# w_down of a squared-ReLU MLP: a seven-product scheme over four pairs of k tiles instead of three, a fifth product that passes from bank to bank, and results added to h by DMA

## The chip, the cores and the metric

The kernel runs on one core of a Trainium2 chip. The metric is device time in microseconds (us) of one execution. TensorE (PE) multiplies, VectorE (DVE) and ScalarE (ACT) do elementwise work, GpSimd (POOL) does little here and issues a few transfers, SyncE (SP) issues the weight loads.

## The reference

A transformer block of width 2048 on 256 rows, in float32. The mixer has two branches (a recurrence and a chunked attention), merged by gates. What the change touches is the MLP behind it, whose hidden width is 8192:

```python
def reference(x, w_in, ..., w_up, w_down, norm_final_w):
    h = x
    h = h + mixer_block(rms_norm(h, norm_mix_w[l]), ..., w_out[l])
    u = rms_norm(h, norm_mlp_w[l])
    h = h + jnp.square(jax.nn.relu(u @ w_up[l])) @ w_down[l]
    return rms_norm(h, norm_final_w)
```

`w_up` is 2048 x 8192, `w_down` is 8192 x 2048.

## The kernel before

**Numbers.** Every float32 operand is split into a high and a low part: `split` (L87) lets ScalarE copy the source into the high part (L89, a cast) and VectorE subtract it from the source (L90). A product of one 128 x 128 block with a 128 x 512 weight tile is then three matmuls of 512 columns (`mm3`, L143 to L145): high by high, high by low, low by high. They add up in a PSUM bank of 128 x 512.

**The MLP.** The hidden width is worked off in four quarters (`qd`, 0 to 3). In a quarter two gemms of 1024 columns each (`up{qd}0`, `up{qd}2`) make the 2048 hidden columns; ScalarE takes each bank through a ReLU and a square. `turn` transposes the results (`tp_u` on TensorE) and splits them into `uT`, tiles named act_u. Then two gemms, `dn{qd}0` and `dn{qd}2`, multiply by the quarter's 2048 rows of w_down, 1024 output columns each, and `out_of` adds each bank to the running sum `h1` (named h in the profile) with one VectorE addition, `evict` (L677). In the last quarter the final norm follows.

**A gemm.** `gemm_s` computes two blocks of 128 rows by two blocks of 512 columns, over 16 k tiles. Four banks `c["11"]`, `c["21"]`, `c["12"]`, `c["22"]` hold the four results. For some pairs of k tiles (k with k+4; r of them) a 2 x 2 by 2 x 2 block product is made with seven products in place of eight, after Winograd. The weight side needs sums of weight blocks, made in place in the raw tiles by VectorE (`add`, L698); the activation side needs combinations S2, S4, S5 and S7, made once for a quarter by `combos`. Products 1 to 7 go to banks, and parts of them move between banks: ScalarE copies a bank (`copy`, L722) to another bank or to a token (a 128 x 512 buffer), and VectorE adds a token to a bank (`more`, L727). The remaining k tiles are plain products, by pairs: `plain` loads 2 tiles of 512 columns and multiplies them by both row blocks.

With r = 3, weight tiles W11, W12, W21, W22 hold two k tiles each, and the third pair lies in X and Y, made of halves. All w_down gemms, w_up gemms (but the first) and gate gemms use r = 3, two others r = 2.

**The order.** Instructions are put in order by a scheduler before the run; each engine then runs its own list in order. `late` and `flush` carry the last plain pair and the last results of a gemm (12 matmuls) into the middle of the next. `turns`, passed as `between`, puts the transposes of the second half of the hidden columns into the first w_down gemm of a quarter.

**Buffers.** A raw weight tile of 128 x 1024 float32 (512 KB) is loaded by one or two DMAs on SyncE's queue (`piece`, L641 and L644). `parts` makes the high and low tiles `wh` and `wl` from it. Raw tiles have eight buffers, 6 in one pool and 2 in another, taken in turn; `wh` and `wl` have six each, by 4 and 2:

```python
BUFS = {"raw": (6, 2), "wh": (4, 2), "wl": (4, 2)}
...
    first = taken[tag] % (old + new) < old
    taken[tag] += 1
```

A raw buffer comes free when the last operation that reads it, mostly a split on VectorE, is done. There are 17 tokens (`TOK`), six PSUM banks for `gemm_s` and two for transposes.

In the names of the profile `wh_dn20p` is the high part of a weight tile for a product of gemm dn20, `wh_dn20r` that of a plain pair, `raw_dn` and `raw_dn20r` the tiles loaded for them, `S_u` an activation combination.

Of the kernel before, what the change touches and what calls it, by code (L numbers as in the profile page):

```python
# [8 lines left out]
F32 = mybir.dt.float32  # L9
F32R = mybir.dt.float32r  # L10
# [6 lines left out]
P = 128  # L17
# [5 lines left out]
NC = 512  # L23
# [27 lines left out]
def tile_hybrid_block(  # L51
# [529 lines left out]

    R = 3

    def combos(lhs, what, home):

        a = []
        for m in range(NM):
            for j in range(2):
                t = tk.tile([P, R, P], F32, name=f"a{m}{j}_{what}", tag="t", bufs=TOK)
                x = lhs[j][:, :R, :, m * P:(m + 1) * P].bitcast(F32)  # L590
                nc.vector.tensor_tensor(t, x[:, :, 0, :], x[:, :, 1, :], op=ALU.add)
                a.append(t)
        a11, a12, a21, a22 = a
        s5 = a22
        nc.vector.tensor_tensor(s5, a21, a22, op=ALU.subtract)
        s7 = a21
        nc.vector.tensor_tensor(s7, a11, a21, op=ALU.subtract)
        s2 = a11
        nc.vector.tensor_tensor(s2, s5, a11, op=ALU.subtract)
        s4 = a12  # L600
        nc.vector.tensor_tensor(s4, a12, s2, op=ALU.add)
        made = {}
        for i, s in ((4, s4), (5, s5), (2, s2), (7, s7)):
            t = (tk if home == "a" else xp).tile([P, R, 2, P], F32R, name=f"S{i}_{what}", tag=f"S{i}{home}", bufs=1)
            split(t[:, :, 0, :], t[:, :, 1, :], s)
            made[i] = t
        return made

    Sx = combos(xT, "x", "a")
# [66 lines left out]
        with tc.high_priority(offset=2000):  # L676
            nc.vector.tensor_tensor(dst, acc, dst, op=ALU.add)  # L677

    def gemm_s(lhs, S, w, n0, what, done, r=R, kt0=0, between=None, fresh=False, tail=False):

        n1 = n0 + NC
        c = {}
        load = lambda name, *halves: piece(w, f"{what}{name}", *[(n, kt0 + k) for n, k in halves])
        W11 = load("11", (n0, 0), (n0, 1))
        if r == 3:
            X = load("x", (n0, 2), (n1, 6))
        W22 = load("22", (n1, 4), (n1, 5))  # L690
        W12 = load("12", (n1, 0), (n1, 1))
        if r == 3:
            Y = load("y", (n0, 6), (n1, 2))
        W21 = load("21", (n0, 4), (n0, 5))

        def add(dst, t):
            with tc.high_priority(offset=2000):
                nc.vector.tensor_tensor(dst, dst, t, op=ALU.add)  # L698

        half = lambda W, i: W[0][:, i * NC:(i + 1) * NC]  # L700

        def mm(i, lh, ps, *tiles):

            first = i not in c
            if first:
                c[i] = bank(f"{what}c{i}")
            wh, wl = ps
            for a, k in tiles:
                mm3(c[i], *lh(k), wh[:, a], wl[:, a], first, False)
                first = False  # L710

        def of(m, jj):
            return lambda k: lhs_of(lhs, k + 4 * jj, m)

        def comb(i):
            return lambda k: [S[i][:, k, u, :] for u in range(2)]

        both = ((0, 0), (1, 1))

        def copy(dst, i):  # L720
            with tc.high_priority(offset=2000):
                nc.scalar.copy(dst, c[i])  # L722
            return dst

        def more(i, t, op):
            with tc.high_priority(offset=2000):
                nc.vector.tensor_tensor(c[i], c[i], t, op=op)  # L727


        p = parts(W11, f"{what}p1")  # L730
        if r == 3:
            px = parts(X, f"{what}px")
        mm("11", of(0, 0), p, *both)
        if r == 3:
            mm("11", of(0, 0), px, (0, 2))
        c["21"] = bank(f"{what}c21")
        if fresh:
            nc.tensor.matmul(c["21"], lhs[0][:, 0, 0, 0:P], lhs[0][:, 0].rearrange("p u t -> p (u t)"), start=True, stop=False, skip_group_check=True)
        copy(c["21"], "11")
        p = parts(W22, f"{what}p3")  # L740
        add(W22[0], W12[0])
        add(W12[0], W11[0])
        mm("12", comb(4), p, *both)
        if r == 3:
            mm("12", comb(4), px, (1, 2))

        p = parts(W12, f"{what}p5")
        mm("22", comb(5), p, *both)
        if r == 3:
            add(half(X, 1), half(Y, 1))  # L750
            add(half(Y, 1), half(X, 0))
            py = parts(Y, f"{what}py")
            mm("22", comb(5), py, (1, 2))
        more("12", copy(token(f"s5_{what}"), "22"), ALU.add)
        if r == 3:
            mm("11", of(0, 1), py, (0, 2))
        p = parts(W21, f"{what}p2")
        mm("11", of(0, 1), p, *both)
        add(W11[0], W22[0])
        flush()  # L760

        p = parts(W11, f"{what}p6")
        mm("21", comb(2), p, *both)
        if r == 3:
            add(half(X, 0), half(X, 1))
            px = parts(X, f"{what}px2")
            mm("21", comb(2), px, (0, 2))
        u1 = copy(token(f"u1_{what}"), "21")

        def plain(n, *ks):  # L770
            p = parts(load(f"r{n}_{ks[0]}", *[(n0 + n * NC, k) for k in ks]), f"{what}r{n}_{ks[0]}")

            def m_half(m):
                for a, k in enumerate(ks):
                    mm3(c["12"[m] + "12"[n]], *lhs_of(lhs, k, m), p[0][:, a], p[1][:, a], False, k == KD - 1)

            return m_half

        def plains(n, *pairs):
            for ks in pairs:  # L780
                p = plain(n, *ks)
                for m in range(NM):
                    p(m)


        left = [(k, k + 1) for k in range(2, KD, 2) if k != 4] if r == 2 else [(3, 7)] + [(k, k + 1) for k in range(8, KD, 2)]
        plains(1, left[0])
        more("12", u1, ALU.subtract)
        p = parts(W22, f"{what}p7")
        mm("21", comb(7), p, *both)  # L790
        if r == 3:
            mm("21", comb(7), px, (1, 2))
        u2 = copy(token(f"u2_{what}"), "21")
        add(W21[0], W11[0])
        early = left[1][1] // 4 < len(lhs)
        if early:
            plains(1, left[1])
        else:
            q = plain(0, *left[0])
            q(0)  # L800
        more("22", u2, ALU.subtract)
        p = parts(W21, f"{what}p4")
        mm("21", of(1, 1), p, *both)
        if r == 3:
            add(half(Y, 0), half(X, 0))
            mm("21", of(1, 1), parts(Y, f"{what}p4y", 0), (0, 2))
        if not early:
            q(1)
        if between:
            between()  # L810

        def end(n):
            for m in range(NM):
                done(m, n, c["12"[m] + "12"[n]])

        plains(0, *left[0 if early else 1:2])
        plains(1, *left[2 if early else 1:2])
        for n in range(2):
            plains(n, *left[2:-3])
        plains(0, *left[max(2, len(left) - 3):])  # L820
        end(0)
        if tail:
            held = [plain(1, *ks) for ks in left[-3:]]
            for m in range(NM):
                for p in held:
                    p(m)
                done(m, 1, c["12"[m] + "2"])
            return
        plains(1, *left[-3:-1])

        def rest():
            plains(1, left[-1])
            end(1)

        late.append(rest)
# [79 lines left out]
    for qd in range(NQ):  # L915
# [4 lines left out]
        def turn():  # L920

            c, rs = pend.pop(0)
            uT.append(new_act(f"u{qd}{c}"))
            hi, lo = uT[-1][:, :, 0, :], uT[-1][:, :, 1, :]
            for m in range(NM):
                tp = transpose4(rs[m], f"u{qd}{c}{m}")
                split(hi[:, :, m * P:(m + 1) * P], lo[:, :, m * P:(m + 1) * P], tp)

        Su = {}

        def turns():
            if len(hT) == 2:
                h_blocks(2)
            while pend:
                turn()
            if len(uT) == 2:
                Su.update(combos(uT, f"u{qd}", "b"))

        for c in range(0, 4, 2):
            rs = {}  # L940
# [14 lines left out]

        def out_of(m, n, acc, last=last):
            r = h1[n][m]
            evict(r, acc)
            if not last:
                return  # L960
            nc.scalar.activation(token(f"ysq_{n}_{m}"), r, AF.Square, accum_out=ssq3[:, m, n:n + 1])
            if n < 3:
                nc.vector.tensor_tensor(r, r, wf[:, n * NC:(n + 1) * NC], op=ALU.mult)
# [12 lines left out]
                (nc.sync if i % 2 else nc.scalar).dma_start(out[m * P:(m + 1) * P, i * NC:(i + 1) * NC], t)  # L976

        for n0 in (0, 2):
            gemm_s(uT, Su, w_down, n0 * NC, f"dn{qd}{n0}", lambda m, n, acc, n0=n0: out_of(m, n0 + n, acc), kt0=qd * KD,
                   between=None if n0 else turns, tail=last and n0 == 2)  # L980


# [42 lines left out]
```

## Time and profile before

| | |
|---|---|
| median of 3 runs | 1426.92 us (1425.85 to 1427.75) |
| the profiled execution | 1427.14 us |
| span of its profile | 1425.4 us |
| mean granted TensorE clock | 0.996 |
| moved by DMA | 272.89 MB |

The span is what the profile sees of one execution; 1.7 us of that execution's time lie around it. Engine times are busy times within the span; a gap of an engine costs time only where the rest waits for it. In rows of groups the columns after the bar are the group's busy time in us and the mean ns of one; in rows of windows, the window, its length, and the busy us and count of instructions of each engine, then the clock, the DMA share and GB/s; in rows of the chain, the start, the length and what ran.

### The profile page before, as it was taken

The numbers are of one execution on the slowest core, as the hardware profiler recorded it, in microseconds if no ns is written. First come the engines' busy times: TensorE is split into PE (matmuls) and PEld (weight loads), VectorE is DVE, ScalarE is ACT, GpSimd is POOL, SyncE is SP. The second block draws the span as 40 slices with busy tenths as digits, with TensorE's granted clock in tenths as the row PEclk, the third lists the DMA queues.
The fourth block names the chain that finished last, engine by engine and source line by source line (L and its number), as shares of the span: only waits on it lengthen the run. The fifth ranks groups of instructions, "written<-read, shape, count | busy, mean of one in ns | idle before, by whom it ended". The sixth has DMA issues, their size and how long they took to land.

```text
span 1425.4 us, 18422 instructions
## 1 busy us (share of the span) xinstructions
PE 1404.7 (99%) x6629; PEld 1163.1 (82%) x6629; DVE 1153.9 (81%) x1522; ACT 849.0 (60%) x1105; POOL 35.5 (2%) x96
## 2 busy tenths in 40 slices
PE   9999999999999999999999999999999999999997
PEld 7878888878787888888888888888888888888886
DVE  7797978675658885688998988889888898889984
ACT  6754844464556664446656765567556775557753
POOL 2000001010000000000000000000000000000000
PEclk9999999999999999999999999999999999999999
DMA  9644554655556557666654576555576555667542
GB/s 327 222 148 147 163 166 142 188 170 168 174 177 221 195 192 228 196 207 222 200 181 134 194 236 209 176 201 169 192 236 232 179 171 170 237 222 237 179 151 99
DMA packets 122156, 272.89 MB, mean 191 GB/s; under 512 B 10176, under 2 KB 31424, under 8 KB 121680
## 3 DMA queue, kind: packets, MB, share of 16 engines
q1 hardware_dynamic: 119328, 264.80, 56.1%
q0 software_dynamic: 1584, 5.31, 1.4%
q10 hardware_dynamic: 1152, 1.60, 0.3%
q8 instruction: 52, 0.85, 0.2%
q14 instruction: 40, 0.33, 0.1%
HBM read 269.57 MB, written 2.10 MB: 191 GB/s over the span
## 4 chain that ended last, share of the span: by engine, by line
PE 83%; DVE 8%; ACT 3%; DMA 3%; issue 2%; POOL 0%; SPq 0%; POOLq 0%; ACTq 0%; DVEq 0%
PE acc_hq L171 2%; PE acc_ak L171 2%; PE acc_aq L171 2%; PE acc_hf L171 2%; PE ps L395 1%; PE acc_bb L143 1%; PE acc_av L144 1%; PE acc_ba L145 1%; PE acc_ba L144 1%; PE acc_ba L143 1%; PE acc_bb L144 1%; PE acc_av L143 1%; PE acc_bb L145 1%; PE acc_av L145 1%; PE acc_ak L170 1%
## 5 line engine op out<-in xcount | busy, mean ns | idle before, releaser
L171 PE MATMUL acc_hf<-act_x,wh_hf 128*128 128x512 f32 x128 | 47.7, 408 | 0.0
L171 PE MATMUL acc_aq<-act_x,wh_aq 128*128 128x512 f32 x128 | 47.5, 406 | 0.0
L171 PE MATMUL acc_hq<-act_x,wh_hq 128*128 128x512 f32 x128 | 46.3, 401 | 0.0
L171 PE MATMUL acc_ak<-act_x,wh_ak 128*128 128x512 f32 x128 | 45.0, 397 | 0.0
L698 DVE TENSOR_TENSOR raw_up<-raw_up,raw_up 128x1024 f32<-128x1024 f32 x32 | 39.0, 1220 | 0.5
L698 DVE TENSOR_TENSOR raw_dn<-raw_dn,raw_dn 128x1024 f32<-128x1024 f32 x32 | 39.0, 1217 | 0.2
L90 DVE TENSOR_TENSOR wl_ga<-raw_ga,wh_ga 128x1024 fp32r<-128x1024 f32 x16 | 19.6, 1225 | 19.6 <-ACT wh_ga L89 18.1
L170 PE MATMUL acc_aq<-act_x,wl_aq 128*128 128x256 f32 x120 | 35.1, 292 | 0.0
L170 PE MATMUL acc_hf<-act_x,wl_hf 128*128 128x256 f32 x120 | 34.5, 287 | 0.0
L90 DVE TENSOR_TENSOR wl_av<-raw_av,wh_av 128x1024 fp32r<-128x1024 f32 x16 | 19.6, 1224 | 18.1 <-ACT wh_av L89 18.1
L170 PE MATMUL acc_ak<-act_x,wl_ak 128*128 128x256 f32 x120 | 33.6, 280 | 0.0
L170 PE MATMUL acc_hq<-act_x,wl_hq 128*128 128x256 f32 x120 | 33.6, 280 | 0.0
L90 DVE TENSOR_TENSOR wl_ba<-raw_ba,wh_ba 128x1024 fp32r<-128x1024 f32 x16 | 19.6, 1223 | 16.6 <-ACT wh_ba L89 16.6
L90 DVE TENSOR_TENSOR wl_bb<-raw_bb,wh_bb 128x1024 fp32r<-128x1024 f32 x16 | 19.5, 1222 | 14.7 <-ACT wh_bb L89 14.7
L89 ACT CAST wh_ba<-raw_ba 128x1024 fp32r<-128x1024 f32 x16 | 16.9, 1053 | 24.3 <-PE acc_ba L145 10.0
L89 ACT CAST wh_bb<-raw_bb 128x1024 fp32r<-128x1024 f32 x16 | 16.9, 1055 | 22.8 <-PE acc_ba L145 12.7
L89 ACT CAST wh_av<-raw_av 128x1024 fp32r<-128x1024 f32 x16 | 16.8, 1052 | 22.0 <-PE acc_av L145 12.4
L171 PEld LDWEIGHTS acc_hq<-act_x,wh_hq 128*128 128x128 f32 x128 | 24.3, 190 | 5.6
L171 PEld LDWEIGHTS acc_hf<-act_x,wh_hf 128*128 128x128 f32 x128 | 24.5, 191 | 5.2 <-DVE f L179 0.3
L89 ACT CAST wh_aq<-raw_aq 128x1024 fp32r<-128x1024 f32 x16 | 16.8, 1049 | 19.7 <-PE acc_aq L171 7.6
L171 PEld LDWEIGHTS acc_ak<-act_x,wh_ak 128*128 128x128 f32 x128 | 23.9, 188 | 5.5
L89 ACT CAST wh_hg<-raw_hg 128x1024 fp32r<-128x1024 f32 x16 | 16.8, 1047 | 19.5 <-PE acc_hg L145 13.3
(1627 smaller groups left out, 5118.1 us busy)
## 6 DMA issues: line engine op xcount, KB each, us to landing
raw_up<-in_w_up_dram SPq DMA_DIRECT2D x32, 512.0 KB, 5.4
raw_dn<-in_w_down_dram SPq DMA_DIRECT2D x32, 512.0 KB, 5.5
raw_ga<-in_w_in_t_dram SPq DMA_DIRECT2D x20, 512.0 KB, 3.7
raw_hi<-in_w_in_n_dram SPq DMA_DIRECT2D x16, 512.0 KB, 4.3
raw_hg<-in_w_in_n_dram SPq DMA_DIRECT2D x16, 512.0 KB, 3.7
raw_aq<-in_w_in_t_dram SPq DMA_DIRECT2D x16, 512.0 KB, 4.3
raw_ak<-in_w_in_t_dram SPq DMA_DIRECT2D x16, 512.0 KB, 3.6
raw_av<-in_w_in_n_dram SPq DMA_DIRECT2D x16, 512.0 KB, 4.4
```

The source lines that it names most:

```text
L89: (copy or nc.scalar.copy)(hi, src)
L90: nc.vector.tensor_tensor(lo, src, hi.bitcast(F32), op=ALU.subtract)
L143: nc.tensor.matmul(acc, hi, wh, start=first, stop=False, skip_group_check=True)
L144: nc.tensor.matmul(acc, hi, wl, start=False, stop=False, skip_group_check=True)
L145: nc.tensor.matmul(acc, lo, wh, start=False, stop=last, skip_group_check=True)
L170: nc.tensor.matmul(acc[:, cb, 0:T], wl[:, c], r[:, 0, :], start=False, stop=False)
L171: nc.tensor.matmul(acc[:, cb, :], wh[:, c], r.rearrange("p u t -> p (u t)"), start=kt == 0, stop=kt == nkt - 1)
L395: nc.tensor.matmul(ps[:, m, :], klf[:, a * P:(a + 1) * P], qrf[:, a * 192:(a + 1) * 192], start=True, stop=True)
L698: nc.vector.tensor_tensor(dst, dst, t, op=ALU.add)
```

## The change

In w_down's gemms r becomes 4: the weight tiles W11, W12, W22 and W21 are two raw tiles of two k tiles each (names with 0 and 2 at the end), there are no X and Y, and the plain pair (3, 7) is gone. `combos` works on four k tiles; the fourth's high and low parts lie in tokens (`S5m`, `S2m`), and its inputs are copies of the transposed blocks made by ScalarE in `turn` in place of sums of high and low on VectorE.

In all gemms of `gemm_s` the products come in the order 1, 5, (the held work of the gemm before), 3, 2, 6, 7, 4 instead of 1, 3, 5, 2, (the held work), 6, 7, 4. Product 5 is made in bank 22, copied by ScalarE into bank 12, and product 3 adds up on top of it (`begun`); before, it was copied to a token and added to bank 12 by VectorE. The sums in the weight tiles change with it: W12 takes W11 first, W22 takes that sum and goes into product 6, and `less` turns W11 into the difference of W22 and W11, which goes into product 7; before, product 6 took W11 and product 7 took W22. The transposes of a w_down gemm are called after product 2 (`soon`) and no longer before the plain products.

In quarters 0 to 2 `out_of` copies a bank to a token on ScalarE, and a DMA from GpSimd's queue adds the token to h; quarter 3 uses `evict` as before.

```diff
@@ -581,15 +581,17 @@
 
     R = 3
 
-    def combos(lhs, what, home):
-
-        a = []
-        for m in range(NM):
-            for j in range(2):
-                t = tk.tile([P, R, P], F32, name=f"a{m}{j}_{what}", tag="t", bufs=TOK)
-                x = lhs[j][:, :R, :, m * P:(m + 1) * P].bitcast(F32)
-                nc.vector.tensor_tensor(t, x[:, :, 0, :], x[:, :, 1, :], op=ALU.add)
-                a.append(t)
+    def combos(lhs, what, home, blocks=None, n=R):
+
+        a = blocks
+        if not a:
+            a = []
+            for m in range(NM):
+                for j in range(2):
+                    t = tk.tile([P, R, P], F32, name=f"a{m}{j}_{what}", tag="t", bufs=TOK)
+                    x = lhs[j][:, :R, :, m * P:(m + 1) * P].bitcast(F32)
+                    nc.vector.tensor_tensor(t, x[:, :, 0, :], x[:, :, 1, :], op=ALU.add)
+                    a.append(t)
         a11, a12, a21, a22 = a
         s5 = a22
         nc.vector.tensor_tensor(s5, a21, a22, op=ALU.subtract)
@@ -600,10 +602,16 @@
         s4 = a12
         nc.vector.tensor_tensor(s4, a12, s2, op=ALU.add)
         made = {}
-        for i, s in ((4, s4), (5, s5), (2, s2), (7, s7)):
-            t = (tk if home == "a" else xp).tile([P, R, 2, P], F32R, name=f"S{i}_{what}", tag=f"S{i}{home}", bufs=1)
-            split(t[:, :, 0, :], t[:, :, 1, :], s)
-            made[i] = t
+        for two in ((5, s5), (4, s4)), ((2, s2), (7, s7)):
+            if n > R:
+                more = tk.tile([P, 2, 2, P], F32R, name=f"S{two[0][0]}m_{what}", tag="t", bufs=TOK)
+            for q, (i, s) in enumerate(two):
+                t = (tk if home == "a" else xp).tile([P, R, 2, P], F32R, name=f"S{i}_{what}", tag=f"S{i}{home}", bufs=1)
+                split(t[:, :, 0, :], t[:, :, 1, :], s[:, :R])
+                made[i] = [[t[:, k, u, :] for u in range(2)] for k in range(R)]
+                if n > R:
+                    split(more[:, q, 0, :], more[:, q, 1, :], s[:, R])
+                    made[i].append([more[:, q, u, :] for u in range(2)])
         return made
 
     Sx = combos(xT, "x", "a")
@@ -676,7 +684,7 @@
         with tc.high_priority(offset=2000):
             nc.vector.tensor_tensor(dst, acc, dst, op=ALU.add)
 
-    def gemm_s(lhs, S, w, n0, what, done, r=R, kt0=0, between=None, fresh=False, tail=False):
+    def gemm_s(lhs, S, w, n0, what, done, r=R, kt0=0, soon=None, between=None, fresh=False, tail=False):
 
 
 
@@ -684,18 +692,17 @@
         n1 = n0 + NC
         c = {}
         load = lambda name, *halves: piece(w, f"{what}{name}", *[(n, kt0 + k) for n, k in halves])
-        W11 = load("11", (n0, 0), (n0, 1))
-        if r == 3:
-            X = load("x", (n0, 2), (n1, 6))
-        W22 = load("22", (n1, 4), (n1, 5))
-        W12 = load("12", (n1, 0), (n1, 1))
-        if r == 3:
-            Y = load("y", (n0, 6), (n1, 2))
-        W21 = load("21", (n0, 4), (n0, 5))
+        groups = (0, 2) if r == 4 else (0,)
+        four = lambda name, n, k: [load(f"{name}{g}", (n, k + g), (n, k + g + 1)) for g in groups]
 
         def add(dst, t):
             with tc.high_priority(offset=2000):
                 nc.vector.tensor_tensor(dst, dst, t, op=ALU.add)
+
+        def less(dst, t):
+
+            with tc.high_priority(offset=2000):
+                nc.vector.tensor_tensor(dst, t, dst, op=ALU.subtract)
 
         half = lambda W, i: W[0][:, i * NC:(i + 1) * NC]
 
@@ -709,63 +716,73 @@
                 mm3(c[i], *lh(k), wh[:, a], wl[:, a], first, False)
                 first = False
 
+        def mms(i, lh, Ws, name):
+            for g, W in zip(groups, Ws):
+                mm(i, lh, parts(W, f"{what}{name}{g}"), (0, g), (1, g + 1))
+
         def of(m, jj):
             return lambda k: lhs_of(lhs, k + 4 * jj, m)
 
         def comb(i):
-            return lambda k: [S[i][:, k, u, :] for u in range(2)]
-
-        both = ((0, 0), (1, 1))
+            return lambda k: S[i][k]
 
         def copy(dst, i):
             with tc.high_priority(offset=2000):
                 nc.scalar.copy(dst, c[i])
             return dst
 
+        def begun(i, j):
+
+            c[i] = bank(f"{what}c{i}")
+            if fresh:
+                nc.tensor.matmul(c[i], lhs[0][:, 0, 0, 0:P], lhs[0][:, 0].rearrange("p u t -> p (u t)"), start=True, stop=False, skip_group_check=True)
+            copy(c[i], j)
+
         def more(i, t, op):
             with tc.high_priority(offset=2000):
                 nc.vector.tensor_tensor(c[i], c[i], t, op=op)
 
 
-        p = parts(W11, f"{what}p1")
+        W11 = four("11", n0, 0)
+        if r == 3:
+            X = load("x", (n0, 2), (n1, 6))
+        W12 = four("12", n1, 0)
+        if r == 3:
+            Y = load("y", (n0, 6), (n1, 2))
+        W22 = four("22", n1, 4)
+        mms("11", of(0, 0), W11, "p1")
         if r == 3:
             px = parts(X, f"{what}px")
-        mm("11", of(0, 0), p, *both)
+            mm("11", of(0, 0), px, (0, 2))
+        begun("21", "11")
+        for a, b in zip(W12, W11):
+            add(a[0], b[0])
+        mms("22", comb(5), W12, "p5")
         if r == 3:
-            mm("11", of(0, 0), px, (0, 2))
-        c["21"] = bank(f"{what}c21")
-        if fresh:
-            nc.tensor.matmul(c["21"], lhs[0][:, 0, 0, 0:P], lhs[0][:, 0].rearrange("p u t -> p (u t)"), start=True, stop=False, skip_group_check=True)
-        copy(c["21"], "11")
-        p = parts(W22, f"{what}p3")
-        add(W22[0], W12[0])
-        add(W12[0], W11[0])
-        mm("12", comb(4), p, *both)
-        if r == 3:
-            mm("12", comb(4), px, (1, 2))
-
-        p = parts(W12, f"{what}p5")
-        mm("22", comb(5), p, *both)
-        if r == 3:
-            add(half(X, 1), half(Y, 1))
             add(half(Y, 1), half(X, 0))
             py = parts(Y, f"{what}py")
             mm("22", comb(5), py, (1, 2))
-        more("12", copy(token(f"s5_{what}"), "22"), ALU.add)
+        begun("12", "22")
+        flush()
+
+        W21 = four("21", n0, 4)
+        mms("12", comb(4), W22, "p3")
+        for a, b in zip(W22, W12):
+            add(a[0], b[0])
         if r == 3:
+            mm("12", comb(4), px, (1, 2))
+            add(half(X, 1), half(Y, 1))
             mm("11", of(0, 1), py, (0, 2))
-        p = parts(W21, f"{what}p2")
-        mm("11", of(0, 1), p, *both)
-        add(W11[0], W22[0])
-        flush()
-
-        p = parts(W11, f"{what}p6")
-        mm("21", comb(2), p, *both)
+        mms("11", of(0, 1), W21, "p2")
+        if soon:
+            soon()
+
+        mms("21", comb(2), W22, "p6")
         if r == 3:
-            add(half(X, 0), half(X, 1))
-            px = parts(X, f"{what}px2")
-            mm("21", comb(2), px, (0, 2))
+            mm("21", comb(2), parts(X, f"{what}px2", 1), (1, 2))
         u1 = copy(token(f"u1_{what}"), "21")
+        for a, b in zip(W11, W22):
+            less(a[0], b[0])
 
         def plain(n, *ks):
             p = parts(load(f"r{n}_{ks[0]}", *[(n0 + n * NC, k) for k in ks]), f"{what}r{n}_{ks[0]}")
@@ -783,15 +800,20 @@
                     p(m)
 
 
-        left = [(k, k + 1) for k in range(2, KD, 2) if k != 4] if r == 2 else [(3, 7)] + [(k, k + 1) for k in range(8, KD, 2)]
+        if r == 2:
+            left = [(k, k + 1) for k in range(2, KD, 2) if k != 4]
+        else:
+            left = [(3, 7)] * (r == 3) + [(k, k + 1) for k in range(8, KD, 2)]
         plains(1, left[0])
         more("12", u1, ALU.subtract)
-        p = parts(W22, f"{what}p7")
-        mm("21", comb(7), p, *both)
+        mms("21", comb(7), W11, "p7")
+        for a, b in zip(W21, W22):
+            add(a[0], b[0])
         if r == 3:
-            mm("21", comb(7), px, (1, 2))
+            less(half(X, 0), half(X, 1))
+            add(half(Y, 0), half(X, 1))
+            mm("21", comb(7), parts(X, f"{what}px3", 0), (0, 2))
         u2 = copy(token(f"u2_{what}"), "21")
-        add(W21[0], W11[0])
         early = left[1][1] // 4 < len(lhs)
         if early:
             plains(1, left[1])
@@ -799,10 +821,8 @@
             q = plain(0, *left[0])
             q(0)
         more("22", u2, ALU.subtract)
-        p = parts(W21, f"{what}p4")
-        mm("21", of(1, 1), p, *both)
+        mms("21", of(1, 1), W21, "p4")
         if r == 3:
-            add(half(Y, 0), half(X, 0))
             mm("21", of(1, 1), parts(Y, f"{what}p4y", 0), (0, 2))
         if not early:
             q(1)
@@ -820,13 +840,13 @@
         plains(0, *left[max(2, len(left) - 3):])
         end(0)
         if tail:
-            held = [plain(1, *ks) for ks in left[-3:]]
+            held = [plain(1, *ks) for ks in left[max(2, len(left) - 3):]]
             for m in range(NM):
                 for p in held:
                     p(m)
                 done(m, 1, c["12"[m] + "2"])
             return
-        plains(1, *left[-3:-1])
+        plains(1, *left[max(2, len(left) - 3):-1])
 
         def rest():
             plains(1, left[-1])
@@ -924,9 +944,13 @@
             hi, lo = uT[-1][:, :, 0, :], uT[-1][:, :, 1, :]
             for m in range(NM):
                 tp = transpose4(rs[m], f"u{qd}{c}{m}")
+                if c < 2:
+                    blocks[m, c] = tk.tile([P, 4, P], F32, name=f"a{m}{c}_u{qd}", tag="t", bufs=TOK)
+                    nc.scalar.copy(blocks[m, c], tp)
                 split(hi[:, :, m * P:(m + 1) * P], lo[:, :, m * P:(m + 1) * P], tp)
 
         Su = {}
+        blocks = {}
 
         def turns():
             if len(hT) == 2:
@@ -934,7 +958,7 @@
             while pend:
                 turn()
             if len(uT) == 2:
-                Su.update(combos(uT, f"u{qd}", "b"))
+                Su.update(combos(uT, f"u{qd}", "b", [blocks[m, j] for m in range(NM) for j in range(2)], 4))
 
         for c in range(0, 4, 2):
             rs = {}
@@ -955,9 +979,13 @@
 
         def out_of(m, n, acc, last=last):
             r = h1[n][m]
+            if not last:
+                t = token(f"y{qd}{n}{m}")
+                with tc.high_priority(offset=2000):
+                    nc.scalar.copy(t, acc)
+                nc.gpsimd.dma_start(r, t, accum_op=ALU.add)
+                return
             evict(r, acc)
-            if not last:
-                return
             nc.scalar.activation(token(f"ysq_{n}_{m}"), r, AF.Square, accum_out=ssq3[:, m, n:n + 1])
             if n < 3:
                 nc.vector.tensor_tensor(r, r, wf[:, n * NC:(n + 1) * NC], op=ALU.mult)
@@ -976,8 +1004,8 @@
                 (nc.sync if i % 2 else nc.scalar).dma_start(out[m * P:(m + 1) * P, i * NC:(i + 1) * NC], t)
 
         for n0 in (0, 2):
-            gemm_s(uT, Su, w_down, n0 * NC, f"dn{qd}{n0}", lambda m, n, acc, n0=n0: out_of(m, n0 + n, acc), kt0=qd * KD,
-                   between=None if n0 else turns, tail=last and n0 == 2)
+            gemm_s(uT, Su, w_down, n0 * NC, f"dn{qd}{n0}", lambda m, n, acc, n0=n0: out_of(m, n0 + n, acc), r=4, kt0=qd * KD,
+                   soon=None if n0 else turns, tail=last and n0 == 2)
 
 
 # ---- launch: one core; inputs and outputs as the reference has them ----
```

## The prediction

> **What bounds the kernel now.** I read the page's totals first, then the chain that ended last.
>
> ```profile
> span 1425.4 us, 18422 instructions
> PE 1404.7 (99%) x6629; PEld 1163.1 (82%) x6629; DVE 1153.9 (81%) x1522; ACT 849.0 (60%) x1105; POOL 35.5 (2%) x96
> PE 83%; DVE 8%; ACT 3%; DMA 3%; issue 2%; POOL 0%; SPq 0%; POOLq 0%; ACTq 0%; DVEq 0%
> ```
>
> TensorE is busy for 1404.7 of 1425.4 us: a matmul less is time won, and a new wait of TensorE is lost in full. But 17% of the chain runs through other engines and DMA: there the weights come only just in time. Next the stretch of the third quarter's first w_down gemm (dn20) by windows, and the same stretch of the chain.
>
> ```profile
> core 0: us, PE busy (x) PEld busy (x) DVE busy (x) ACT busy (x) POOL busy (x), PEclk, DMA share, GB/s
> 1145.00:1165.00 20.00, 20.00 (x92) 16.57 (x91) 19.92 (x24) 15.17 (x21) 0.00 (x0) 1.00 0.26 82
> 1165.00:1185.00 20.00, 19.93 (x95) 16.37 (x94) 17.36 (x19) 14.37 (x20) 0.00 (x0) 1.00 0.85 287
> ```
>
> ```profile
> 1161.12 1.13 DVE wl_up22r L90
> 1162.25 1.14 DVE raw_dn L698
> 1163.39 1.14 DVE wl_dn20p L90
> 1164.55 0.33 SPq L644
> 1164.93 3.88 DMA raw_dn20r<-in_w_down_dram
> 1168.91 1.05 ACT wh_dn20r L89
> ...
> 1174.61 5.64 DMA raw_dn20r<-in_w_down_dram
> ```
>
> TensorE is full, VectorE has 0.08 us free in the first window. The chain shows one loop: a split on VectorE frees a raw buffer (DVE wl_dn20p), SyncE issues the load that waited for it (0.33), the tile lands 3.88 later, ScalarE casts it (1.05), VectorE makes its low part. Today TensorE has 20 us of other products around this loop.
>
> **The matmuls.** Two rows of the timeline stand for a run of equal matmuls; seven spacings lie between them.
>
> ```profile
> 1157.91 0.39 PE L143 MATMUL acc_dn20c<-wh_dn20p,act_u 128*128 128x512 f32 x1
> ...
> 1159.50 0.39 PE L144 MATMUL acc_dn20c<-wl_dn20px,act_u 128*128 128x512 f32 x1
> ```
>
> 1.59/7 = 0.227 us each. Every w_down gemm has one product of three matmuls less (183 to 180), 24 over eight gemms; two gate gemms get one opening matmul each more. So 22 x 0.227 = 5.0 us less. The counts are fixed by the program, so this part does happen.
>
> **VectorE and ScalarE.** Durations by form:
>
> ```profile
> L698 DVE TENSOR_TENSOR raw_dn<-raw_dn,raw_dn 128x1024 f32<-128x1024 f32 x32 | 39.0, 1217 | 0.2
> L90 DVE TENSOR_TENSOR wl_dn20r<-raw_dn20r,wh_dn20r 128x1024 fp32r<-128x1024 f32 x10 | 12.1, 1221 | 2.4 <-ACT wh_dn20r L89 2.0
> L89 ACT CAST wh_dn20p<-raw_dn 128x1024 fp32r<-128x1024 f32 x7 | 7.4, 1051 | 3.4 <-PE acc_up22c L145 2.4 <-ACT S_u L89 0.5 <-PE acc_dn20c L145 0.5
> L677 DVE TENSOR_TENSOR h<-acc_dn20c,h 128x512 f32<-128x512 f32 x4 | 2.7, 683 | 0.0
> L727 DVE TENSOR_TENSOR acc_dn20c<-acc_dn20c,u_dn 128x512 f32<-128x512 f32 x2 | 1.4, 693 | 0.0
> L722 ACT COPY u_dn<-acc_dn20c 128x512 f32<-128x512 f32 x2 | 1.2, 582 | 0.0
> h<-in_x_dram POOLq DMA_DIRECT2D x8, 256.0 KB, 4.3
> ```
>
> VectorE loses 21 bank additions (x 0.69) and 24 additions into h (x 0.68), and 16 sums of transposed blocks; it gains 32 weight sums of 1.22 in place of 32 half ones, and more splits: a few us less in all. ScalarE gains some 38 us (24 result copies and 16 block copies at 0.58, and casts) at 60% load. Costed at nothing, because TensorE's matmuls cover both engines in the mean; the order within a gemm is another matter, below. The copy of the fifth product into the next bank (0.58) is covered by the held 12 matmuls of the gemm before (12 x 0.227 = 2.7 us); without the cover, as in a gemm that has no predecessor to finish, it shows with up to 0.6.
>
> The 24 accumulating transfers (256 KB each, 6.3 MB) are not in the trace. Nearest is the load of x, 4.3 us from issue. Each h tile is added to again a quarter later, so their latency is free; their bandwidth is 2% of the 272.9 MB moved. Bounds 0 and, if each delays one weight load by its own 4.3 us and all of it shows, 103; I take 0, nearest to the low DMA share of 0.26 in the first window.
>
> [...]
>
> **The new wait.** Weights pass through eight raw buffers: six of one pool, two of another, taken in a fixed order. Up to now a w_down gemm holds six tiles and three half pairs come and go; W21's load waits for an old plain pair and is early. With four pairs a gemm holds eight tiles (W11, W12, W22, W21, each in two halves a and b), and the last plain pair of the gemm before needs a ninth buffer. In the changed program W11a, W21a and W21b all fall to the pool of two. So W21b's load waits on SyncE until VectorE has read one of the others for the last time: W11a's split for the seventh product (six gemms), or W21a's split for the fourth (dn12, dn20). Every load behind W21b on SyncE waits too; ScalarE and VectorE have the second product's splits of W21b in front of the first plain pair's, and TensorE has little but the sixth product to do meanwhile.
>
> ```profile
> 1201.24 1.22 DVE L90 TENSOR_TENSOR wl_dn22p<-raw_dn,wh_dn22p 128x1024 fp32r<-128x1024 f32 x1
> ...
> 1204.65 1.22 DVE L90 TENSOR_TENSOR wl_dn20r<-raw_dn20r,wh_dn20r 128x1024 fp32r<-128x1024 f32 x1
> ```
>
> Three starts further is 3.41 us, so VectorE's 1024-wide operations follow 1.14 apart. I count from the start of the first product.
> - dn12: TensorE ends the sixth product's first half after 60 matmuls (13.6). That frees the buffer for the cast of W21a's sum: cast 1.05, split 1.22 and the hops end at 16.1. Issue 0.33 and landing 3.88 and hops: 20.45. Cast to 21.65, split ready at 23.0. TensorE wants it after 68 matmuls, 15.4: stall 7.6.
> - dn20: the same behind the last transposes, ready at 24.5, wanted at 16.95: 7.6.
> - dn22: VectorE is dense from 1.3; ten 1024-wide operations later (11.4) W11a's last split ends at about 12.9. Landed 17.3, ready 19.7, wanted 15.4: 4.3.
> - the same count along the program's order, with the end of W11a's last split: dn30 and dn00 13.4 (ready 20.2, wanted 17.55) 2.65 each; dn10 14.3, 1.3; dn32 16.6, 3.9; dn02 15.4, 2.8.
>
> Sum 7.6 + 7.6 + 4.3 + 5.3 + 1.3 + 3.9 + 2.8 = 32.8 us. The landing is the weak number; w_down's plain loads, for dn20 and then dn22:
>
> ```profile
> DMA to landing us min/median/max: 3.5/4.5/6.0
> DMA to landing us min/median/max: 3.0/4.8/7.4
> ```
>
> From issue the chain's is 4.2. With 3.0 each stall is 1.2 shorter, 23 in all; with 6.0 each is 1.8 longer, 47. I take the chain's, since this load, too, is issued late and alone.
>
> [...]
>
> **The rest.** In gate, w_out and w_up gemms with three pairs, W11 is now kept until the seventh product, and the first late plain pair waits for a split near 11.4: ready at 18.2 where TensorE wants it at 17.7. So 0 to 0.5 in each of 12 gemms, 1.8 more with a slow load; I take 0.25, 3 us. Against that one wait goes, or part of it:
>
> ```profile
> PE acc_ga2c L143 <- ACT wh_ga2p L89: 1.6, 1, 1.6
> ```
>
> ga2 begins with everything late; the fifth product, which now comes second, needs W12 alone. 0 to 1.6, I take 0.7. At the end of the last quarter two plain pairs stand in place of three before each half closes: 12 matmuls, 2.7 us, over an addition and a square of under 0.7 each. Nothing.
>
> **Sum.** The profiled execution took 1427.14 us (span 1425.4), 0.2 above the median. 1427.1 - 5.0 - 0.7 + 32.8 + 3 = 1457.2: **1457 us**, 2.1% slower. About 0.2% (2.9 us) is what a measurement of this kernel can tell from no change.
>
> **Rivals.**
> - *The loads land in time* (faster). W21b's loop costs 4.2 + 1.05 + 1.22 + hops, 6.8 us, from the split that frees the buffer. If TensorE has 6.8 us of work there, nothing stalls: 1427.1 - 5.7, 1421.4, up to 1424.4 with the 3 us of the other gemms. That speaks for it that the chain above has just such a loop without a TensorE gap. Against it: I count 68 matmuls up to the wish in dn12, 8 after the event that starts its loop, 1.8 us against 9.4. It decides where cover passes loop, which no gemm does by my count. Chance 0.08.
> - *Only dn12 and dn20 stall.* W11a's split is not tied to TensorE's sixth product; if VectorE runs 4 us ahead of my count, the six others vanish: 1421.4 + 15.2, 1437. The second window's 17.36 of 20 shows that VectorE has some slack. Chance 0.15.
> - *Slow loads.* Landing takes 6.0, because transfers released together and the accumulations collide: 1421.4 + 47 + 3, 1471. The 5.64 in the chain and 0.85 of DMA share are for it, 0.26 in the other window against. Chance 0.15.
> - *Gain and stalls cancel*, to within 0.2%: stalls of 3 to 8 us in all. It needs the two tied gemms to stall for 4 where the bare loop takes 9.4 against 1.8. Chance 0.02.
>
> **How the numbers follow.** Forecast 0.60, which takes in landings from 3.5 to 5. The range reaches from the second rival (1436) to just over the third (1474); outside lie the first, the fourth, and the ends of the others. Faster 0.08, same 0.02, slower 0.90.
>
> **What would show it.** In the changed kernel's profile: w_down's gaps of TensorE before the second product's second half, 3 to 8 us, eight of them; ScalarE's casts of dn tiles waiting for "DMA raw_dn" with the same lengths; TensorE's busy time about 5 us lower (1400) and a span some 30 longer, the difference within the four w_down stretches and none of it in the branches. I am wrong if W21b's loads land before TensorE wants them, if TensorE finds other matmuls to run in its program's order, or if TensorE waits for the bank copies or VectorE's sums in place of a load.

## The result, and the profile after

| | before | after |
|---|---|---|
| median | 1427.34 us (1425.85 to 1427.95, 4 runs) | 1488.6 us (1486.98 to 1490.84, 4 runs) |
| profiled execution | 1427.14 | 1487.29 |
| its span | 1425.4 | 1485.6 |
| mean granted TensorE clock | 0.996 | 0.984 |

The ratio is 1.0439 (95% interval 1.0426 to 1.0451): slower by 61 us, where 1457 was forecast with a range up to 1474. The direction was right; the loss forecast (30 us) was half of the loss measured.

The totals of the page after:

```profile
span 1485.6 us, 18389 instructions
...
PE 1422.1 (96%) x6607; PEld 1166.9 (79%) x6607; DVE 1156.7 (78%) x1496; ACT 887.2 (60%) x1180; POOL 54.4 (4%) x120
...
PE 78%; DVE 8%; DMA 7%; ACT 4%; issue 2%; POOL 0%; SPq 0%; POOLq 0%; DVEq 0%; ACTq 0%
```

TensorE has 22 matmuls less (6607 for 6629) and yet is busy 17.4 us longer; and it idles 63.5 us (1485.6 less 1422.1) in place of 20.7. So there are two losses, 42.8 us of idle time and 22.4 us by which the same matmuls take longer (17.4 and the 5.0 saved): 42.8 + 22.4 - 5.0 is the 60.2 us of the two spans.

Who TensorE waited for, from the MLP and what leads to it (sum, times, longest):

```profile
PE tp_u L106 <- DVE act_u L90: 7.6, 4, 2.7
PE acc_dn12c L143 <- ACT wh_dn12p L89: 5.8, 1, 5.8
PE acc_dn20c L143 <- ACT wh_dn20p L89: 5.4, 1, 5.4
PE acc_dn22c L143 <- ACT wh_dn22p L89: 4.4, 2, 4.2
PE acc_dn32c L143 <- ACT wh_dn32p L89: 3.7, 2, 3.5
...
PE tp_h L106 <- DVE hw L910: 3.1, 2, 2.0
PE acc_dn00c L143 <- ACT wh_dn00p L89: 2.4, 2, 2.0
PE acc_dn30c L143 <- ACT wh_dn30p L89: 2.2, 2, 1.8
PE acc_dn02c L143 <- ACT wh_dn02p L89: 1.8, 2, 1.6
PE acc_up30c L143 <- ACT wh_up30r L89: 1.3, 1, 1.3
...
PE acc_dn10c L143 <- ACT wh_dn10p L89: 1.1, 1, 1.1
...
PE acc_up12c L144 <- DVE wl_up12r L90: 0.8, 1, 0.8
```

All eight w_down gemms wait for a product's cast: 26.8 us by these rows. Beside them stand waits that the forecast did not have, of the transposes (`tp_u`, `tp_h`, 10.7). What stands behind dn12's 5.8 is read in the chain:

```profile
1062.03 0.24 PE acc_dn12c L145
1062.34 1.06 ACT wh_dn12p L89
1063.42 1.24 DVE wl_dn12p L90
1064.67 3.63 DMA raw_dn<-in_w_down_dram
1068.33 1.05 ACT wh_dn12p L89
1069.40 0.92 DVE wl_dn12p L90
1070.33 0.04 issue
1070.37 0.79 PE acc_dn12c L143
1071.16 0.43 PE acc_dn12c L144
1071.59 0.43 PE acc_dn12c L145
...
1075.86 0.34 PE acc_dn12c L144
1076.19 0.23 PE acc_dn12c L145
```

This is the loop of the prediction, step by step: TensorE ends the sixth product's first half, the cast of W21a's sum, its split, which frees the raw buffer, W21b's load, its cast, its split. Then comes what the prediction did not have: twelve matmuls from 1070.37 on are 0.43 and more apart, twice the 0.23 of before. The windows around the two longest gaps name the reason, a mean granted clock below 1:

```profile
1050.00:1075.00 25.00, 19.04 (x73) 14.95 (x72) 18.18 (x16) 12.72 (x15) 1.70 (x2) 0.81 0.52 148
1200.00:1225.00 25.00, 19.42 (x77) 15.24 (x76) 17.97 (x18) 15.30 (x18) 0.00 (x0) 0.86 0.57 185
```

Over the span the clock not granted comes to 0.016 x 1485.6 = 23.8 us, before 0.004 x 1425.4 = 5.7; 18.1 more, a part of it while TensorE waited anyway. The trace records when the clock changes: in the MLP, up to the last matmul, it stands at 0.50 in seven stretches of 3.41 to 10.24 us, where the profile before has none. Their sum as windows:

```profile
sum 37.56, PE 31.77 PEld 24.27 DVE 30.94 ACT 21.87 POOL 0.00; mean PE 4.54 PEld 3.47 DVE 4.42 ACT 3.12 POOL 0.00
```

TensorE is busy in 31.8 us of them. In the chain above the matmuls are 0.43 apart at a clock of 0.50, and 0.23 from 1076.19 on, so I estimate that some half of it, 15.9 us, is lost. The other 6.5 of the 22.4 I put down to how idle time is read, an estimate not shown gap by gap: a matmul behind a gap shows 0.39 to 0.50 us where in a row it shows 0.23, and there are some 30 gaps more.

### The profile page after: what moved, and what is told of

Same layout as the page of the kernel before. It is cut to its first block, busy times and chain, and to the rows that moved or that the text cites. A ratio compares the mean times of both kernels' runs of the same rounds, so it can differ in the third digit from the quotient of the medians.

```text
span 1485.6 us, 18389 instructions
## 1 busy us (share of the span) xinstructions
PE 1422.1 (96%) x6607; PEld 1166.9 (79%) x6607; DVE 1156.7 (78%) x1496; ACT 887.2 (60%) x1180; POOL 54.4 (4%) x120
## 4 chain that ended last, share of the span: by engine, by line
PE 78%; DVE 8%; DMA 7%; ACT 4%; issue 2%; POOL 0%; SPq 0%; POOLq 0%; DVEq 0%; ACTq 0%
DMA raw_dn<-in_w_down_dram 4%; PE acc_ak L171 2%; PE acc_hq L171 2%; PE acc_aq L171 2%; PE acc_hf L171 2%; PE ps L395 1%; PE acc_bb L143 1%; PE acc_ba L145 1%; PE acc_av L143 1%; PE acc_bb L144 1%; PE acc_ba L144 1%; PE acc_bb L145 1%; PE acc_ba L143 1%; PE acc_av L144 1%; PE acc_av L145 1%
## 5 line engine op out<-in xcount | busy, mean ns | idle before, releaser
L700 DVE TENSOR_TENSOR raw_dn<-raw_dn,raw_dn 128x1024 f32<-128x1024 f32 x48 | 58.6, 1221 | 2.9 <-DMA raw_dn<-in_w_down_dram 2.6
L986 POOL DMA_DIRECT2D h<-y x24 | 20.4, 851 | 513.4 <-ACT y L985 513.1
L90 DVE TENSOR_TENSOR wl_ga<-raw_ga,wh_ga 128x1024 fp32r<-128x1024 f32 x16 | 19.6, 1225 | 18.1 <-ACT wh_ga L89 16.6
L90 DVE TENSOR_TENSOR wl_av<-raw_av,wh_av 128x1024 fp32r<-128x1024 f32 x16 | 19.6, 1224 | 18.1 <-ACT wh_av L89 18.1
L700 DVE TENSOR_TENSOR raw_up<-raw_up,raw_up 128x1024 f32<-128x1024 f32 x24 | 29.3, 1222 | 4.5 <-DMA raw_up<-in_w_up_dram 3.3
```

Source lines behind the costliest of these rows:

```text
L90: nc.vector.tensor_tensor(lo, src, hi.bitcast(F32), op=ALU.subtract)
L986: nc.gpsimd.dma_start(r, t, accum_op=ALU.add)
```

## The experiments

Times are medians; the kernel before, beside them on the same chip, had 1425.88 us (first four), 1426.6 (next four) and 1426.3 (last two).

**1. The same memory, other buffers.** The eight raw buffers stay; only which tile takes which changes.

```diff
-        raw = buf("raw", F32, what)
...
+        early_ones = {2: ("120", "110", "220"), 3: ("120", "110", "x", "y", "220"), 4: ("120", "122", "110", "112", "220", "222")}[r]
+        place = {k: room_for(f"{what}{k}", 0) for k in early_ones}
+        beside = {2: (10, 11, 12), 3: (3, 9, 10), 4: (7, 8)}[r]
...
+                new = 1 if name[0] != "r" or plain_no[0] in beside else 0
+                raw = room_for(f"{what}{name}", new)
```

`early_ones` take buffers of the pool of six ahead of their loads, in that order. Of the rest W21 and the plain pairs numbered in `beside`, the last of them the held one, take the pool of two (`new`), the other plain pairs the pool of six again, so that the first of them follow W12.

> The changed kernel with the eight raw buffers handed out in another order: W12, W11 and W22 take the pool of six, W21b takes the buffer of the held last plain pair and no longer that of W11a or W21a; late plain pairs take W12's buffers first. Same instructions, same memory. Theory (raw buffers kept too long cause the gaps of TensorE, directly before the second product and, through late plain pairs, at the transposes and in w_up, and the half clock follows the gaps): nearly all gaps and all half-clock stretches of the MLP go, time 1422 to 1440 us. Rival (order of casts and sums on ScalarE and VectorE, bank copies or the accumulating transfers make the gaps): the gaps stay, 1480 us or more.

1426.53 us (1425.01 to 1428.9, 10 runs), ratio 1.0002 (0.9993 to 1.0012). The whole loss is gone, with the same matmuls, casts and sums on every engine. Their order is not quite the same: some 230 of the 6607 matmuls stand elsewhere in TensorE's list. The experiment does not separate this from the buffers. TensorE's waits in the MLP are now:

```profile
PE tp_h L106 <- DVE hw L927: 1.8, 2, 1.1
...
PE tp_u L106 <- DVE act_u L90: 0.8, 1, 0.8
...
PE acc_dn30c L143 <- ACT u_dn L748: 0.5, 1, 0.5
PE acc_dn00c L143 <- ACT u_dn L748: 0.4, 1, 0.4
```

(with two more of 0.4), and TensorE's busy time is down as it should be:

```profile
span 1423.9 us, 18415 instructions
...
PE 1400.2 (98%) x6607; PEld 1157.8 (81%) x6607; DVE 1152.9 (81%) x1496; ACT 886.3 (62%) x1180; POOL 56.5 (4%) x120
```

1404.7 - 1400.2 = 4.5 us, close to the 5.0 of the 22 matmuls. As the theory had it: raw buffers held too long made the gaps, and the half clock of the MLP went with them: the profile's mean granted clock is 0.996 again, that of before, where the change had 0.984.

**2. Three pairs in w_down, all else as changed.**

```diff
-                Su.update(combos(uT, f"u{qd}", "b", [...], 4))
+                Su.update(combos(uT, f"u{qd}", "b", [...]))
...
-            gemm_s(uT, Su, w_down, ..., r=4, kt0=qd * KD, ...)
+            gemm_s(uT, Su, w_down, ..., kt0=qd * KD, ...)
```

> The changed kernel with w_down at three pairs again (one more product per gemm), all else as changed: new order of products, bank to bank, block copies by ScalarE, accumulation by DMA. Theory (raw buffers): the W21b gaps (29 us shown before the second products and just behind them) and their half clock (11) go, 5 us of matmuls come back, the gaps at transposes and in w_up stay: 1440 to 1455 us. Rival (new order or accumulating transfers cost by themselves): 1480 us or more.

1449.02 us (1447.83 to 1450.77), ratio 1.016 (1.0143 to 1.0177). As expected. No second product waits any more, but the waits of transposes stay:

```profile
PE tp_u L106 <- DVE act_u L90: 8.7, 5, 2.3
PE tp_h L106 <- DVE hw L910: 5.3, 2, 3.4
```

So the change costs some 23 us with the old order of buffers even without the fourth pair, and the other order of buffers takes them away (experiment 6). Its other parts were not taken out one by one here; the new order of products, which keeps W11 until the seventh, is the likely one.

**3. No accumulating transfers.**

```diff
+            evict(r, acc)
             if not last:
...
-                    nc.scalar.copy(t, acc)
-                nc.gpsimd.dma_start(r, t, accum_op=ALU.add)
                 return
-            evict(r, acc)
```

> The changed kernel with the w_down results added to h by VectorE in all quarters, no accumulating transfers. Theory (raw buffers): same as the changed kernel within 5 us, 1484 to 1494 us. Rival (accumulating transfers slow the weight loads): 10 us or more faster.

1485.38 us (1484.04 to 1493.24), ratio 1.0429 (1.04 to 1.0458); the change itself had 1.0439, and the intervals overlap. The 24 transfers are not the cause.

**4. Useless work in two of the gaps.**

```diff
+        p6 = mms("21", comb(2), W22, "p6")
+        if what in ("dn12", "dn20"):
...
+            for i in range(22):
+                nc.tensor.matmul(junk, p6[0][:, 1, 0:P], ..., start=not i, stop=i == 21, ...)
```

> The changed kernel with 22 useless matmuls (5.0 us at full clock) in each of dn12 and dn20, placed where TensorE waits 5.8 and 5.4 us for W21b; their result is not used. Theory (a gap of this length lowers the granted clock for some 6.5 us behind it, which costs 3.3 us each on top of the gap): the useless work makes the kernel 5 to 7 us faster, near 1482 us, and the half clock at these two places goes. Rival (the gap alone counts): 1488 us or slower.

1481.34 us (1479.65 to 1485.34), ratio 1.0393 (1.0373 to 1.0414) against 1.0439: some 6.6 us faster, with 44 matmuls more. In the timeline, the matmul that first uses W21b in dn12, after the change and in this kernel (in brackets the idle time before it):

```profile
1069.42 0.79 PE L143 MATMUL acc_dn12c<-wh_dn12p,act_u 128*128 128x512 f32 x1 [5.81 <-ACT wh_dn12p L89]
```

```profile
1062.78 0.49 PE L143 MATMUL acc_dn12c<-wh_dn12p,act_u 128*128 128x512 f32 x1 [0.73 <-ACT wh_dn12p L89]
```

And the window around it in this kernel:

```profile
1045.00:1070.00 25.00, 23.81 (x105) 19.14 (x104) 18.30 (x17) 13.30 (x16) 1.70 (x2) 1.00 0.52 150
```

The data arrive as late as before, but the clock stays at 1.00, and by the chain the matmuls behind are 0.23 apart from 1064.68 on, not 0.43. From the last matmul of the sixth product to the first of the seventh it is 11.06 us in place of 13.73 in dn12, and 10.75 in place of 13.35 in dn20. So the half clock is a price of its own: 2.6 to 2.7 us for each of these two gaps by the traces, 3.3 by the medians.

**5. Other buffers in w_down alone.**

```diff
-        place = {k: ...}
+        place = {} if r != 4 else {k: ...}
...
+                raw = room_for(...) if r == 4 else buf("raw", F32, ...)
```

> The changed kernel with the other order of raw buffers in w_down's gemms alone; gate, w_out and w_up gemms take them as in the changed kernel. This splits the 62 us that the new order of buffers gave back. Theory (two sources: W21b in w_down with 29 us of gaps and some 13 of half clock; late plain pairs in the other gemms with 14 us of gaps at transposes and w_up and 5 of half clock): 1440 to 1450 us. Rival (W21b is the only source and the gaps elsewhere follow from it): within 4 us of the kernel with all buffers reordered, 1423 to 1430 us.

1435.82 us (1431.16 to 1437.77), ratio 1.0057 (1.0038 to 1.0077): below what was expected. Of the 62 us, the buffers in w_down's gemms account for 53 (1488.6 to 1435.8), those in the other gemms for 9. (The edit moves w_down's plain pairs as well as W21b.) I had given w_down 42: some gaps in w_up that I had put down to late plain pairs (up30's 1.3 and 0.8, up20's 0.8) are gone here too, so they followed from w_down; that its late loads hold up SyncE's queue into the next gemm is the likely way, not tried by itself. The transposes still wait:

```profile
PE tp_u L106 <- DVE act_u L90: 5.9, 4, 3.2
...
PE tp_h L106 <- DVE hw L927: 2.9, 2, 1.8
```

**6 to 8. What is left when buffers are in time.** Each on top of 1: three pairs in w_down; additions by VectorE; block sums by VectorE in place of ScalarE's copies. The edits of 6 and 7 are those of 2 and 3; that of 8:

```diff
-                    nc.scalar.copy(blocks[m, c], tp)
+                    nc.vector.tensor_tensor(blocks[m, c], hi[...], lo[...], op=ALU.add)
```

> The changed kernel with the other order of raw buffers everywhere and w_down at three pairs. It has 24 matmuls more than the kernel with that order and four pairs, 5.4 us. Theory (with buffers in time only TensorE's work counts): 1429 to 1433 us, 3 to 7 us above the four-pair kernel of the same buffers. Rival (four pairs bring waits of their own that eat the matmuls): no more than 1 us above it, or below it.

> The changed kernel with the other order of raw buffers everywhere and w_down's results added to h by VectorE in all quarters. Theory (accumulating transfers cost nothing, VectorE has room): 1424 to 1428 us, the same as with transfers. Rival (VectorE is too full for 24 more additions of 0.68): 2 us or more slower; other rival (transfers disturb the loads): 2 us or more faster.

> The changed kernel with the other order of raw buffers everywhere and the transposed blocks for the combinations again made by VectorE as sums of high and low part, without ScalarE's 16 copies. Theory (what is left of gaps, 4.4 us, comes from VectorE's order and short bank copies, not from ScalarE's block copies): within 2 us, 1424 to 1429 us. Rival (the block copies keep the transposes' banks too long): 2 us or more faster.

1426.89 us (ratio 1.0005, 0.9995 to 1.0015), 1426.83 (1.0004, 0.9993 to 1.0015) and 1427.32 (1.001, 1.0 to 1.002). 7 and 8 came as the theory had it. 6 is a miss: three pairs, with 24 matmuls more, are no slower than four beyond what can be resolved. Three pairs' profile has none of the four waits for `u_dn`, a bank copy of ScalarE (0.45 each), and a shorter end. The last matmul starts at 1413.63 with four pairs (experiment 1) and at 1415.46 with three; from there to the end of the span it is 10.3 us (1423.9) with four, 9.4 (1424.9) with three. So by these two profiles, of 5.4 us, 3.6 are lost before the last matmul, of which the four waits with the matmuls behind them explain an estimated 2.4 (4 x 0.6), and 0.8 behind it. One us remains in the spans, and it does not show in the medians.

**9 and 10. Can the rest be had?** On top of 7: one plain pair of the last gemm is moved so that three pairs close each half; then also the transposes ahead of the second product.

```diff
-        if early:
+        swap = tail and r == 4
+        if swap:
+            plains(0, left[0])
+        elif early:
             plains(1, left[1])
...
-            held = [plain(1, *ks) for ks in left[max(2, len(left) - 3):]]
+            held = [plain(1, *ks) for ks in left[1 if swap else max(2, len(left) - 3):]]
```

```diff
+        if soon:
+            soon()
         mms("11", of(0, 1), W21, "p2")
-        if soon:
-            soon()
```

> The kernel with buffers reordered and additions on VectorE, in whose last gemm one plain pair changes places, so that three pairs and no longer two close each half (18 matmuls, 4.1 us, beside the first half's closing work). Theory (two pairs are too short a cover at the end: 10.3 us lie between the last matmul and the end with four pairs, 9.4 with three): that stretch is 9.4 again and the time 0.5 to 1 us lower, 1424 to 1427 us, below what the comparison can resolve. Rival (the end does not depend on it): the stretch stays at 10.3.

> The same, and in w_down's gemms the transposes are called before the second product, not after it, so that they do not stand between the products that wait for bank copies. Theory: the four gaps of 0.45 before the fourth product go or shrink, 1 to 2 us less than the kernel before it, 1422 to 1426 us, at the edge of a difference from the kernel before the change. Rival (the transposes then wait for ScalarE and VectorE, which are full at that place): new gaps at the transposes, 1426 us or more.

1426.49 us (ratio 1.0008, 0.9996 to 1.0019) and 1428.77 (1.002, 1.0011 to 1.0028). In 9 the end takes 10.0 us (last matmul at 1415.84 of 1425.8) against 10.7 in 7 (1412.80 of 1423.5): 0.7 of the 0.9 expected, too little to show in the time. In 10 the waits for `u_dn` shrink only from 0.45 to 0.34, and new ones come, as the rival said:

```profile
PE acc_dn20c L143 <- DVE acc_dn20c L760: 2.2, 1, 2.2
PE tp_u L106 <- DVE act_u L90: 2.1, 4, 0.9
```

No version tried is faster than the kernel before.

## Why the prediction was wrong

- **The matmuls** (5.0): right as far as can be told. With buffers in time TensorE is busy 4.5 us less in experiment 1; over 1, 7, 8, 9 and 10, with the same matmuls, it is 2.2 to 6.4 (1402.5 to 1398.3).
- **The new wait** (32.8): right in its mechanism and nearly in its size. The gaps before the second product, with the short ones right behind them (0.15 to 0.53), add up to 29 us. Gemm by gemm, forecast and the longest wait of the rows above: dn12 7.6 and 5.8, dn20 7.6 and 5.4, dn22 4.3 and 4.2, dn32 3.9 and 3.5, dn02 2.8 and 1.6, dn00 2.65 and 2.0, dn30 2.65 and 1.8, dn10 1.3 and 1.1. The order is the same but for dn02. The large ones were too large because the loop took 8.1 us (1062.3 to 1070.4) where I had counted 9.4, and because TensorE goes on when the cast is done, a split's 0.92 before I let it. The landing, the weak number, was 3.6 in dn12, 3.5 in dn20 and 4.7 to 5.4 in the other six, by rows that include the issue, against 4.2. There the slower landing about makes up for the 0.92; only dn02's stall is clearly shorter than counted, and why stays open.
- **The step that failed: a gap was priced at its own length.** The prediction multiplied matmuls by 0.227 us everywhere, and TensorE does not run at one rate: behind the longer gaps the matmuls are 0.43 apart. This cost an estimated 15.9 us in all, and the prediction had no term for it. I had read only windows with a clock of 1.00, and did not ask what my own gaps would do to it. The profile before had a case of it, ahead of the MLP, where TensorE waits 2.9 us (`ps`, L395):

```profile
79.71:83.12 3.41, 0.47 (x4) 0.45 (x4) 3.41 (x9) 1.52 (x3) 0.00 (x0) 1.00 0.51 157
83.12:86.53 3.41, 3.41 (x11) 3.13 (x11) 2.54 (x11) 1.05 (x2) 0.00 (x0) 0.50 0.51 154
```

- **The rest in the other gemms** (3): mis-sized and put in the wrong place. The late tiles did not only make their own matmuls wait. In the longest of the transposes' six waits ScalarE stood at a cast whose tile had not landed, and the transposes' bank copies stood behind it in ScalarE's order:

```profile
800.66 1.05 ACT L89 CAST wh_up02r<-raw_up02r 128x1024 fp32r<-128x1024 f32 x1 [2.11 <-DMA raw_up02r<-in_w_up_dram]
802.95 1.04 ACT L89 CAST wh_up02r<-raw_up02r 128x1024 fp32r<-128x1024 f32 x1 [1.25 <-DMA raw_up02r<-in_w_up_dram]
804.38 0.59 ACT L89 CAST act_u<-tp_u 128x512 fp32r<-128x512 f32 x1
805.91 0.79 PE L106 MATMUL tp_u<-ident,r 128*128 128x128 f32 x4 [2.66 <-DVE act_u L90]
```

  At 1360.98, behind a wait of 1.83, it was the same: ScalarE waited 2.38 for `raw_up32r`. In the other four waits it was VectorE, by the chain: it stood at a weight sum whose tile landed late, with an operation behind it that the transposes needed, as at 754.71 (1.95 us):

```profile
753.36 0.69 DVE L700 TENSOR_TENSOR raw_up02y<-raw_up02y,raw_up02x 128x512 f32<-128x512 f32 x1 [0.55 <-DMA raw_up02y<-in_w_up_dram]
753.97 0.68 DVE L910 TENSOR_TENSOR hw<-tp_h,vt 128x512 f32<-128x512 f32 x1
```

  The transposes wait 7.6 and 3.1 us in all, none of which I had; the other gemms' products wait some 3.6, all in w_up, near the 3 forecast. I asked who consumes the late tile, and not what else is queued behind its cast or its sum.
- **Costed at nothing**: the accumulating transfers rightly so (3 and 7), and the block copies too (8). The end was not nothing: 0.8 us with two closing pairs for three.
- **The rivals**: none describes what happened. "Slow loads" had a time nearer to the result (1471), but its cause did not occur: no load of W21b took the 6.0 that it needs, 5.4 was the longest.

Taken together, the spans are 60.2 us apart where the forecast had 30.1. Of the 30 between, the half clock is 16. The other 14 are waits: 11 at transposes and 6 by which gaps read too short (matmuls that read long behind them), less the 4 by which W21b's gaps fell short of the forecast. The remaining us is open.

## What to carry to other kernels

Count the buffers that a stage holds at once against those that a pool has, and name the tile whose buffer the next load takes: eight buffers were enough here, and handing them out in another order was worth 62 us with no work added or taken away. A gap of the matrix engine cost more than its length here where the clock fell behind it (2.6 to 2.7 us more at each of the two longest), so price both, and when a load is late, list everything that stands behind its first readers on their engines. And a saving of 5 us in 1427 needs every cover that it shortens to be looked at, since two closing pairs in place of three and four waits of 0.45 were enough to eat most of it.

## What the runs showed of the hardware that I had not expected

The clock falls after shorter gaps than I would have guessed, and not after each. Behind the gap of 1.95 us at 754.71 the changed kernel's next matmuls are 0.43 apart, seven in a row; behind 1.97 us at 844.01 they run at 0.23. So it isn't the length alone.

The recorded clock of the two profiles, before and after, shows where it fell. It is 1.00 or 0.50, and it changes only at points that lie whole multiples of 3.41 us apart; half clock in the MLP after the change lasts one, two or three times 3.41. Here are three such windows of the changed kernel, each with the one behind it:

```profile
751.69:755.10 3.41, 1.46 (x9) 0.96 (x8) 2.86 (x5) 1.42 (x4) 0.00 (x0) 1.00 0.51 173
755.10:758.51 3.41, 3.41 (x11) 2.73 (x10) 2.65 (x5) 2.07 (x5) 0.00 (x0) 0.50 0.42 142
840.44:843.85 3.41, 1.60 (x7) 0.95 (x6) 1.33 (x2) 1.52 (x2) 0.00 (x0) 1.00 0.25 91
843.85:847.26 3.41, 2.81 (x11) 1.95 (x12) 3.27 (x3) 3.41 (x5) 0.00 (x0) 1.00 0.02 5
1304.65:1308.06 3.41, 1.32 (x5) 0.77 (x5) 1.95 (x3) 3.03 (x4) 0.00 (x0) 1.00 0.92 322
1308.06:1311.47 3.41, 3.41 (x10) 2.64 (x9) 3.28 (x3) 1.86 (x3) 0.00 (x0) 0.50 0.87 277
```

In the first pair TensorE is idle for 1.95 of 3.41 us, and the next window runs at 0.50. In the second a boundary cuts the gap of 1.97, 1.81 of it lie in one window, and the clock stays. In the third two gaps of 1.32 and 0.77, with matmuls between them, add up to 2.09, and the clock falls. I divided the two profiles at these points, from 30 us on and up to 10 us before the last matmul. All 9 full-clock windows in which TensorE was idle for 1.95 us or more were followed by one at half clock, and none of the 800 with 1.81 or less. What sets the clock these traces do not show.
